# Forms of x made in the attention's output projection, and two more pairs of the feed-forward part computed by seven products

## The chip, the cores and the metric

The kernel runs on one core of one Trainium2 chip. The metric is the device time of one execution in microseconds (us). Times are medians of several runs; the profile comes from one execution, and its span reaches from the first to the last instruction.

The engines are named as the profile names them: PE is TensorE's matmul, PEld its weight load, DVE VectorE, ACT ScalarE, POOL GpSimd, SP the engine whose queue issues most loads. A name with a q (SPq, POOLq) is that engine's queue.

## The reference

Two layers work on one sequence of 512 tokens of 1024 features in float32. Each has a mixer (attention in layer 0, an mLSTM in layer 1), a cross-attention to a memory of 256 tokens, and a gated feed-forward part with a causal convolution of three taps. What bears on the change:

```python
def memory_cross_attention(xn, memn, wq, wkv, wo):
    q = split_heads(xn @ wq, XATTN_HEADS)
    k, v = jnp.split(memn @ wkv, 2, axis=-1)
    ...
    p = jax.nn.softmax(logits, axis=-1)
    out = jnp.einsum('bhqm,bhmd->bhqd', p.astype(v.dtype), v)
    return merge_heads(out) @ wo

def conv_ffn(xn, w_up, conv_w, conv_b, w_down):
    h = causal_depthwise_conv(xn @ w_up, conv_w) + conv_b
    g, u = jnp.split(h, 2, axis=-1)
    return (jax.nn.gelu(g) * u) @ w_down

    ...
        x = x + memory_cross_attention(rms_norm(x, xattn_norm[layer]), rms_norm(mem, mem_norm[layer]),
                                       xattn_wq[layer], xattn_wkv[layer], xattn_wo[layer])
        x = x + conv_ffn(rms_norm(x, ffn_norm[layer]), ffn_w_up[layer], ffn_conv_w[layer],
                         ffn_conv_b[layer], ffn_w_down[layer])
```

The inner width of the feed-forward part is 2816, so w_up makes 2 x 22 blocks of 128 features: 22 pairs of a gate block and an up block.

## The kernel before

**Products.** x lies with its features on the 128 partitions, in 8 tiles of 128 x 512. Every operand is split into a high part, rounded to the reduced float32 that TensorE reads (fp32r), and the low rest; a product is three matmuls, high by high, high by low and low by high (`mm3`, lines 347 to 349). So each 128 x 1024 slice of weights is loaded from memory (`raw`, three buffers), cast to its high part on ScalarE (`wh`) and subtracted to its low part on VectorE (`wl`; three buffers each). The profile shows all ScalarE, VectorE and GpSimd instructions under line 269, the wrapper that issues them, so they are told apart by their tiles.

**Cross-attention** (`xattn`). Keys (`kth`, `ktl`) and values (`xvh`, `xvl`) of the memory, four tiles of 8 KB a partition in the pool `xa`, are read by the scores and the weighted sums of four heads. Then `p_out` multiplies by the output weights in eight blocks m = 0 to 7 of 24 matmuls of 512 columns. After each, VectorE adds the block to x (`xadd`), ScalarE and VectorE make the high and low part of that x tile times the norm's gain (`xprep`: xh, xl) and add its squares for the next norm. A planner (`Plan`) sets the order of this part by priorities and assumed engine times.

**Feed-forward part** (`ffn_steps`). A planner (`Sched`) simulates the engines with assumed durations and fixes the order on TensorE, VectorE, ScalarE and GpSimd; SP's loads are placed by it, with loads allowed to run 14 us ahead, and are then issued in order by the queue. There are two ways to compute a pair:

- `plain`: gate block and up block, 8 slices of features each, 3 matmuls of 512 columns a slice: 48 matmuls. VectorE splits two weight tiles and evacuates two blocks times the norm.
- `seven`: the pair is a 2 x 2 product of blocks (gate and up by the two halves of the features, against the two halves of the features by the two halves of the tokens) computed with seven products of 256 columns in place of eight (4 slices x 3 matmuls each, 84 matmuls). It needs sums of weight blocks, which are made by loading and by adding transfers that GpSimd issues (`sa`, `sb`), one sum on VectorE, five splits of weights, and combinations of x, which are here called the forms: for feature tiles k and k + 4, T1 to T4 are differences of halves of both, 128 x 1024 together, split into `th` and `tl`. Results are combined in `hs` and multiplied by the norm.

After either, the `tail` runs the convolution (one ScalarE and two VectorE instructions a block), the gelu, the product and its split into `ah` and `al`. `SEVEN` (line 26) names the pairs by seven: 4 to 21 in both layers. The forms are made by `forms(k, at)` for k = 0 to 3, two after pair 0 and two after pair 1, with scratch in the tiles s2 and s4 and in `sa`; `th`, `tl` are 32 KB a partition in the pool `ff`. From pair 5 on, a pair by seven is interleaved with two fills (`fill`): blocks of the down projection of a chunk of earlier pairs, 12 matmuls of 512 columns each, whose results are added to x. The first fill uses pairs 0 to 3. Some fills are held back at the end (six in layer 0, four in layer 1), so the last pairs run without.

**Pools.** `xa` and `ff` follow each other in the same address range, and `mem`, which holds the output projection's operands of heads 2 and 3, lies at the start of the range that `ff` takes over. With `reuse_waits="tile"` a tile of the later pool waits only for the earlier tiles whose bytes it takes.

Of the kernel before, what the change touches and what calls it, by code (L numbers as in the profile page):

```python
# [1 line left out]

# [7 lines left out]
F32 = mybir.dt.float32  # L10
# [6 lines left out]
P = 128  # L17
# [8 lines left out]
SEVEN = (range(4, 22), range(4, 22))  # L26
# [269 lines left out]
class Builder:  # L296
# [25 lines left out]

    def acc_bank(self, b):
        return self.til(self.acc, f"acc{b}", bufs=1)
# [155 lines left out]
    def p_out(self, pl, src, mixed, kdeps, gain, gi, order, prio, reload=False, order0=None):  # L480

        state = {}
        done = []
        for m in range(KB8):
            e = self.p_proj(
                pl, src[m], mixed, lambda ps, m=m: self.xadd(m, ps, reload), (("D", 0.6),), kdeps=kdeps, order=order, prio=prio + m
            )
            done.append(
                pl.add(lambda m=m: self.xprep(m, gain, gi, state), 0, [e], prio + m, chain=(("A", 0.52), ("D", 0.66), ("A", 0.52)), order=[order0])
            )  # L490
        self.state = state
        self.xdone = {k: [d] for k, d in enumerate(done)}
# [634 lines left out]
    def xattn(self, layer):  # L1127
        nc, t, tc = self.nc, self.t, self.tc
        with tc.tile_pool(name=f"xa{layer}", bufs=1, reuse_waits="tile") as mp:
            self.mp = mp  # L1130
            pl = Plan(self.plan, [st["banks"][0] for st in self.fills], s=2, w=2, e=4, q=2, pt=2, wt=3)
            self.pad(mp, 192)
# [9 lines left out]
            for h in range(4):  # L1142
                p = 10 + 10 * h
                ke = []
                for m in (2 * h, 2 * h + 1):

                    def keys(ps, m=m, at=0):
                        tmp = self.til(mp, "tmp")
                        nc.vector.tensor_tensor(out=folded(tmp[:, :MEM]), in0=restored(ps[:, at : at + MEM]), in1=folded(self.memrb[:]), op=ALU.mult)
                        self.split(kth[:, m, :], ktl[:, m, :], tmp[:, :MEM])  # L1150
# [32 lines left out]
                if h % 2 == 0:  # L1183
                    cs = slice(256 * h, 256 * h + 512)

                    def values(tk, ps, cs=cs):
                        self.evac_tok(ps, self.memr[:, tk : tk + 1], vh[:, tk, cs], vl[:, tk, cs])
# [10 lines left out]
                for i in range(4):  # L1198
# [3 lines left out]
                    def score(h=h, qs=qs, res=res, sl=sl):  # L1202
                        sp = self.bank("s")
                        for d in range(2):
                            kb = 2 * h + d
                            self.mm3(sp[:, :MEM], qs[d][0][:, sl], qs[d][1][:, sl], kth[:, kb, :], ktl[:, kb, :], d == 0, d == 1)
# [22 lines left out]
                for d in range(2):  # L1229

                    def weigh(h=h, d=d, pts=pts):
                        c = slice(256 * h + P * d, 256 * h + P * d + P)
                        ps = self.bank("w")
                        for j in range(2):
                            self.mm3(ps[:], vh[:, j, c], vl[:, j, c], pts["h"][:, j, :], pts["l"][:, j, :], j == 0, j == 1)
# [7 lines left out]
            self.p_out(pl, t["xo"][layer], lambda: (mh, ml), kd, "ffn", layer, None, 100)  # L1243
# [8 lines left out]
    def ffn_steps(self, layer, mp):  # L1252
# [4 lines left out]
        sc = Sched(raw=3, h=3, s2=1, s4=1, a22=1, sa=3, sb=2, ra=2, hs=2, c=1, ft=2, v=1, u2=1, u3=1, act=10, acc=4, s=2, w=2)  # L1257
# [68 lines left out]
        add("DVE", 1.3, None, (), -20.0, after=1.8)  # L1326
        own = lambda k: (self.xh[k][:], self.xl[k][:])
# [32 lines left out]
        th, tl = ([mp.tile([P, 1024], F32R, name=f"t{i}{layer}{k}", tag=f"t{i}{k}") for k in range(4)] for i in "hl")  # L1360
        formed, pads = [], []
# [3 lines left out]

        def forms(k, at):

            st = {}

            def scaled(j):  # L1370
                st["t"] = st.get("t", ()) + (self.til(mp, ("s2", "s4")[st["_ft"]] + "hl"[j], bufs=1),)
                nc.scalar.activation(st["t"][j][:], self.x[k + 4 * j][:], AF.Identity, scale=self.col("ffn", layer * 8 + k + 4 * j))

            def first():
                st["r"] = raw_tile(st, "sa")[:]
                tt_(out=st["r"][:, T1], in0=st["t"][0][:, 0:256], in1=st["t"][0][:, 256:512], op=ALU.subtract)
                tt_(out=st["r"][:, T3], in0=st["t"][1][:, 256:512], in1=st["t"][0][:, 256:512], op=ALU.subtract)

            def second(to, a, b):
                nc.vector.scalar_tensor_tensor(out=st["r"][:, to], in0=st["r"][:, a], scalar=-1.0, in1=st["t"][1][:, b], op0=ALU.mult, op1=ALU.subtract)  # L1380

            T1, T3, T2, T4 = (slice(256 * i, 256 * i + 256) for i in range(4))
            tt_ = nc.vector.tensor_tensor
            a = add("ACT", ACV, lambda: scaled(0), (), at, [("ft", st)], after=X_LAST)
            a = add("ACT", ACV, lambda: scaled(1), [a], at)
            a = add("DVE", 2 * tt(256), first, [a], at, [("sa", st)])
            a = add("DVE", 0.4, lambda: second(T2, T1, slice(256, 512)), [a], at)
            a = add("DVE", 0.4, lambda: second(T4, T2, slice(0, 256)), [a], at, (), [("ft", st)])
            h = add("ACT", act(1024), lambda: nc.scalar.copy(th[k][:], st["r"]), [a], at)
            formed.append(add("DVE", tt(1024), lambda: self.sub(tl[k][:], st["r"], th[k][:]), [h], at, (), [("sa", st)]))  # L1390

# [66 lines left out]
        def seven(p, fill):  # L1458
# [75 lines left out]
            p6 = pe(n, lambda: product(s2, 0, *T2, "Y", False), [w2, v, *formed], (), [("s2", s2)])  # L1534
# [25 lines left out]
        def down(c, m, steps=1):  # L1560
# [22 lines left out]
            e = add("DVE", 0.6, lambda: self.xadd(m, d["ps"]), [last, xadded[m], *formed], clock[0] + 3.0, (), [("w", d)])  # L1583
# [10 lines left out]
        for p in range(22):  # L1594
# [6 lines left out]
            if p < 2:  # L1601
# [416 lines left out]
```

## Time and profile before

| | us |
|---|---|
| median of 3 runs | 1415.94 |
| lowest and highest | 1414.96, 1417.21 |
| the profiled execution's own time: its span, the only time that the profile gives of it | 1413.6 |
| median less span | 2.3 |
| TensorE busy | 1401.1 (99%) |
| VectorE busy | 1140.9 (81%) |
| ScalarE busy | 825.8 (58%) |
| GpSimd busy | 124.8 (9%) |
| moved | 190.02 MB, mean 134 GB/s |

Consecutive records of an engine overlap in the profile: a VectorE instruction's record ends after the next one has begun. Where pace matters, the distance from start to start is read, not the length of a record; busy times of a stage count overlapping time once. A matmul's record is longer than its pitch for the same reason, so small gaps of TensorE are found from starts and counts.

Layer 0's feed-forward part begins at 393.66 us and layer 1's at 1076.61 us.

### The profile page before, as it was taken

To read this page: it belongs to the slowest core of one execution; us is meant where nothing else is said; L and a number is where in the kernel's file an instruction comes from. 1 tells how busy PE (TensorE), PEld (TensorE's weight loads), DVE (VectorE), ACT (ScalarE), POOL (GpSimd) and SP (SyncE) were. 2 spreads that over 40 slices of the span, in tenths; PEclk is the share of its full clock that TensorE was granted. 3 is DMA by queue.
4 is the path that set the end of the run, shared out by engine and by line. 5 is a ranking of instruction groups with operands and counts; after the bars stand their busy time and mean duration, and the time that the engine had idled before them with its cause. 6 is when DMAs were issued, how large, how long until landed. Compare 5 with 4: busy or idle time off the path is not lost.

```text
span 1413.6 us, 22281 instructions
## 1 busy us (share of the span) xinstructions
PE 1401.1 (99%) x8448; PEld 1262.1 (89%) x8448; DVE 1140.9 (81%) x1922; ACT 825.8 (58%) x1386; POOL 124.8 (9%) x189
## 2 busy tenths in 40 slices
PE   9999999999999999999999999999999999999998
PEld 8888868899889999999888888989988999999997
DVE  7787886766699999999768876666667999999984
ACT  6797564444476656566446664445446656656655
POOL 0002220000001111110001121000000110111000
PEclk9999999999999999999999999999999999999999
DMA  5214324323258767774233332333323876767522
GB/s 206 90 55 155 112 83 147 123 81 129 89 155 211 195 179 185 183 177 114 77 114 102 129 97 83 121 102 120 120 82 134 202 205 169 193 172 189 141 76 81
DMA packets 69212, 190.02 MB, mean 134 GB/s; under 512 B 7553, under 2 KB 7553, under 8 KB 69105
## 3 DMA queue, kind: packets, MB, share of 16 engines
q1 hardware_dynamic: 55648, 153.48, 32.5%
q0 software_dynamic: 12448, 34.00, 13.6%
q8 instruction: 66, 1.08, 0.3%
q10 hardware_dynamic: 1008, 1.12, 0.2%
q14 instruction: 42, 0.34, 0.1%
HBM read 186.43 MB, written 2.15 MB: 133 GB/s over the span
## 4 chain that ended last, share of the span: by engine, by line
PE 88%; DVE 5%; ACT 3%; issue 2%; DMA 1%; POOL 0%; POOLq 0%; DVEq 0%; ACTq 0%
PE acc L347 18%; PE acc L348 18%; PE acc L349 17%; PE w L347 5%; PE w L349 5%; PE w L348 5%; PE s L347 3%; PE s L349 3%; PE s L348 3%; PE acc L409 2%; PE acc L411 2%; PE acc L410 2%; DVE wl L269 1%; PE w L1794 1%; PE w L1027 1%
## 5 line engine op out<-in xcount | busy, mean ns | idle before, releaser
L269 ACT CAST wh<-raw 128x1024 fp32r<-128x1024 f32 (+2 forms) x229 | 235.0, 1027 | 211.2 <-PE acc L348 114.0
L269 DVE TENSOR_TENSOR wl<-raw,wh 128x1024 fp32r<-128x1024 f32 (+2 forms) x229 | 273.8, 1197 | 43.6 <-ACT wh L269 42.9
L347 PE MATMUL acc<-xh,wh 128*128 128x512 f32 (+1 forms) x800 | 275.8, 345 | 0.0
L349 PE MATMUL acc<-xh,wl 128*128 128x512 f32 (+1 forms) x800 | 273.4, 342 | 0.0
L348 PE MATMUL acc<-xl,wh 128*128 128x512 f32 (+1 forms) x800 | 273.2, 342 | 0.0
L349 PEld LDWEIGHTS acc<-xh,wl 128*128 128x128 f32 x800 | 152.1, 190 | 13.7
L347 PEld LDWEIGHTS acc<-xh,wh 128*128 128x128 f32 x800 | 152.2, 190 | 12.6 <-DVE x L269 0.3
L348 PEld LDWEIGHTS acc<-xl,wh 128*128 128x128 f32 x800 | 152.2, 190 | 12.2
L269 DVE SCALAR_TENSOR_TENSOR c<-hs,vec,c 128x512 f32<-128x512 f32 x176 | 131.7, 748 | 3.8 <-ACT c L269 0.8
L347 PE MATMUL w<-ah,wh 128*128 128x512 f32 x304 | 115.7, 381 | 0.2 <-ACT c L269 0.2
L348 PE MATMUL w<-al,wh 128*128 128x512 f32 x304 | 115.2, 379 | 0.0
L349 PE MATMUL w<-ah,wl 128*128 128x512 f32 x304 | 115.2, 379 | 0.0
L269 ACT ACTIVATE c<-hs,vec 128x512 f32<-128x512 f32 x88 | 70.9, 812 | 10.3 <-DVE hs L269 5.9
L269 ACT CAST ah<-c 128x512 fp32r<-128x512 f32 x44 | 27.2, 618 | 83.8 <-DVE c L269 83.8
L269 DVE TENSOR_TENSOR x<-acc,x 128x512 f32<-128x512 f32 (+1 forms) x43 | 28.0, 652 | 56.3 <-PE acc L349 56.3
L347 PEld LDWEIGHTS w<-ah,wh 128*128 128x128 f32 x304 | 57.6, 190 | 7.9 <-DVE x L269 0.9
L349 PEld LDWEIGHTS w<-ah,wl 128*128 128x128 f32 x304 | 57.5, 189 | 8.1
L348 PEld LDWEIGHTS w<-al,wh 128*128 128x128 f32 x304 | 57.6, 190 | 6.5
L349 PE MATMUL acc<-mem,wl 128*128 128x256 f32 (+1 forms) x192 | 59.6, 310 | 1.1 <-DVE wl L269 1.1
L347 PE MATMUL acc<-mem,wh 128*128 128x256 f32 (+1 forms) x192 | 59.6, 310 | 0.1
L348 PE MATMUL acc<-mem,wh 128*128 128x256 f32 (+1 forms) x192 | 59.5, 310 | 0.0
L269 POOL DMA_DIRECT2D sa<-in_up_dram x36 | 31.8, 883 | 276.8 <-DMA sa<-in_up_dram 174.5
(365 smaller groups left out, 3762.0 us busy)
## 6 DMA issues: line engine op xcount, KB each, us to landing
raw<-in_up_dram SPq DMA_DIRECT2D x52, 512.0 KB, 3.9
sa<-in_up_dram SPq DMA_DIRECT2D x36, 512.0 KB, 3.4
sa<-in_up_dram POOLq DMA_DIRECT2D x36, 512.0 KB, 6.5
raw<-in_down_dram SPq DMA_DIRECT2D x32, 512.0 KB, 3.8
ra<-in_up_dram SPq DMA_DIRECT2D x36, 256.0 KB, 4.0
sb<-in_up_dram POOLq DMA_DIRECT2D x36, 256.0 KB, 4.8
raw<-in_wo_dram SPq DMA_DIRECT2D x16, 512.0 KB, 3.9
raw<-in_xk_dram SPq DMA_DIRECT2D x16, 512.0 KB, 3.3
```

The costliest lines, as they stand in the source:

```text
L269: i = issue(*a, **k)
L347: mm(out, wh, xh, start=first, stop=False, skip_group_check=parts)
L348: mm(out, wh, xl, start=False, stop=False, skip_group_check=parts)
L349: mm(out, wl, xh, start=False, stop=last, skip_group_check=parts)
L409: mm(ps, xh[k][:, ts], wh, start=(k == 0), stop=False)
L410: mm(ps, xh[k][:, ts], wl, start=False, stop=False)
L411: mm(ps, xl[k][:, ts], wh, start=False, stop=(k == 7))
L1027: nc.tensor.matmul(ps[64 * s : 64 * s + 64, j * P : 512], v[j][:, c : c + 64], pts[s]["t"][:, at : at + 512 - j * P], start=(j == 0), stop ...
L1794: nc.tensor.matmul(ps[:, lo:], vv[s][:, c], a[:], start=(s == 0), stop=(s == 3))
```

## The change

- Keys, values and forms share one pool `far`, placed from the other end of the memory: eight tiles of 128 x 1024 (`far_tiles`). Keys and values are sliced out of them; when the attention has read them, the same tiles are asked for again for `th` and `tl`. The four old tiles of `xa` and the eight of `ff` go, and three paddings with them.
- `p_out` of the cross-attention takes its blocks in the order 0, 4, 1, 5, 2, 6, 3, 7 and makes the form of tiles k and k + 4 (`form`) as soon as both are done, with scratch in `tmp` and `pth` of the attention's pool. The instructions of a form are the same as before: two scalings, four differences, a cast and a subtraction.
- `forms` in the feed-forward part goes; the planner there counts the last form as work that is already under way.
- Pairs 2 to 21 instead of 4 to 21 are computed by seven.
- `finish` takes its output tiles from `far`.

```diff
-SEVEN = (range(4, 22), range(4, 22))
+SEVEN = (range(2, 22), range(2, 22))
...
+    def far_tiles(self):
+
+        return [self.til(self.far, f"f{i}", (P, 1024), F32R, bufs=1) for i in range(8)]
...
-    def p_out(self, pl, src, mixed, kdeps, gain, gi, order, prio, reload=False, order0=None):
+    def p_out(self, pl, src, mixed, kdeps, gain, gi, order, prio, reload=False, order0=None, forms=None):
...
-        for m in range(KB8):
+        for n, m in enumerate((0, 4, 1, 5, 2, 6, 3, 7) if forms else range(KB8)):
...
+            done[m] = pl.add(lambda m=m: self.xprep(m, gain, gi, state), 0, [e], prio + n, chain=(("A", 0.52), ("D", 0.66), ("A", 0.52)), order=[order0])
+            if forms and m >= 4:
+                if m == 4:
+                    self.forms = [None] * 4
+                pl.add(
+                    lambda k=m - 4: self.form(forms, gi, k), 0, [done[m - 4], done[m]], prio + n,
+                    chain=(("A", 1.22), ("D", 1.4), ("A", 0.95), ("D", 1.14)),
+                )
...
+    def form(self, pool, layer, k):
+
+        nc = self.nc
+        if k == 0:
+            self.far_forms = self.far_tiles()
+        hi, lo = self.far_forms[2 * k : 2 * k + 2]
+        v = [self.til(pool, "tmp"), self.til(pool, "tmp")]
+        for j in range(2):
+            nc.scalar.activation(v[j][:], self.x[k + 4 * j][:], AF.Identity, scale=self.col("ffn", layer * 8 + k + 4 * j))
+        r = self.til(pool, "pth", (P, 2, 512), F32R)[:].rearrange("p a b -> p (a b)").bitcast(F32)
+        T1, T3, T2, T4 = (r[:, 256 * i : 256 * i + 256] for i in range(4))
+        x0, x1 = ([v[j][:, 256 * i : 256 * i + 256] for i in range(2)] for j in range(2))
+        nc.vector.tensor_tensor(out=T1, in0=x0[0], in1=x0[1], op=ALU.subtract)
+        nc.vector.tensor_tensor(out=T3, in0=x1[1], in1=x0[1], op=ALU.subtract)
+        nc.vector.scalar_tensor_tensor(out=T2, in0=T1, scalar=-1.0, in1=x1[1], op0=ALU.mult, op1=ALU.subtract)
+        nc.vector.scalar_tensor_tensor(out=T4, in0=T2, scalar=-1.0, in1=x1[0], op0=ALU.mult, op1=ALU.subtract)
+        self.split(hi[:], lo[:], r)
+        self.forms[k] = hi, lo
...
-            kth = mp.tile([P, KB8, MEM], F32R, name=f"kth{layer}")
-            ktl = mp.tile([P, KB8, MEM], F32R, name=f"ktl{layer}")
-            self.pad(mp, 64)
-            vh = mp.tile([P, 2, DM], F32R, name=f"xvh{layer}")
-            vl = mp.tile([P, 2, DM], F32R, name=f"xvl{layer}")
+            tiles = self.far_tiles()
+            kt = lambda part, m: tiles[2 * part + m // 4][:, m % 4 * MEM : m % 4 * MEM + MEM]
+            vt = lambda part, j, c: tiles[4 + 2 * part + j][:, c]
...
-            self.p_out(pl, t["xo"][layer], lambda: (mh, ml), kd, "ffn", layer, None, 100)
+            self.p_out(pl, t["xo"][layer], lambda: (mh, ml), kd, "ffn", layer, None, 100, forms=mp)
...
+        f = add("ACT", 1.22, None, (), -20.0, after=2.4)
+        f = add("DVE", 1.4, None, [f], -20.0)
+        f = add("ACT", 0.95, None, [f], -20.0)
+        formed = add("DVE", 1.14, None, [f], -20.0)
...
-        th, tl = ([mp.tile([P, 1024], F32R, name=f"t{i}{layer}{k}", tag=f"t{i}{k}") for k in range(4)] for i in "hl")
-        formed, pads = [], []
+        th, tl = zip(*self.forms)
+        pads = []
...
-            p6 = pe(n, lambda: product(s2, 0, *T2, "Y", False), [w2, v, *formed], (), [("s2", s2)])
+            p6 = pe(n, lambda: product(s2, 0, *T2, "Y", False), [w2, v, formed], (), [("s2", s2)])
...
-            if p < 2:
-                for k in (2 * p, 2 * p + 1):
-                    forms(k, clock[0] + 4.0 * (k % 2))
...
-                with tc.tile_pool(name=f"mem{layer}", bufs=1, reuse_waits="tile") as self.memp:
-                    (self.mix0, self.mix1)[layer]()
-                    self.xattn(layer)
-                self.ffn(layer)
+                with ExitStack() as right:
+                    with tc.tile_pool(name=f"mem{layer}", bufs=1, reuse_waits="tile") as self.memp:
+                        (self.mix0, self.mix1)[layer]()
+                        self.far = right.enter_context(tc.tile_pool(name=f"far{layer}", bufs=1, side="right", reuse_waits="tile"))
+                        self.xattn(layer)
+                    self.ffn(layer)
```

More of the change, by code (lines that the diff above doesn't have):

```diff
@@ L1 @@
 import math
+from contextlib import ExitStack
 import numpy as np
@@ L1364, in ffn_steps @@
             nc.gpsimd.memset(h[:, :, 0:2], 0.0)
[L1366 to L1390, printed above, removed]
         def tail(p, st, deps, at):
@@ L1582, in down @@
                     joined([last], last.prio, [("act", acted[first + k].st)])
-            e = add("DVE", 0.6, lambda: self.xadd(m, d["ps"]), [last, xadded[m], *formed], clock[0] + 3.0, (), [("w", d)])
+            e = add("DVE", 0.6, lambda: self.xadd(m, d["ps"]), [last, xadded[m]], clock[0] + 3.0, (), [("w", d)])
             xadded[m] = e
@@ L1847, in finish @@
         HALF = [slice(0, 256), slice(256, 512)]
-        outs = [self.til(mp, f"t{i}{k}", (P, 1024), F32R, bufs=1).bitcast(F32)[:, s] for k in range(4) for i in "hl" for s in (slice(0, 512),)]
+        outs = [v[:].bitcast(F32)[:, 0:512] for v in self.far_tiles()]
         def add(m, ps, c):
```

20 lines of the change are left out of this document (8 added, 12 removed).

## The prediction

> **What bounds the kernel now.** I read the page first, then the busy time by stage, then TensorE's and VectorE's timelines at the start of layer 0's feed-forward part, then the chain of waits at its end.
>
> ```profile
> span 1413.6 us, 22281 instructions
> PE 1401.1 (99%) x8448; PEld 1262.1 (89%) x8448; DVE 1140.9 (81%) x1922; ACT 825.8 (58%) x1386; POOL 124.8 (9%) x189
> ...
> PE 88%; DVE 5%; ACT 3%; issue 2%; DMA 1%; POOL 0%; POOLq 0%; DVEq 0%; ACTq 0%
> ```
>
> TensorE is busy for 99% of the span and 88% of the chain that ended last is its own work, so shortening it should show, if what feeds it keeps up. That is read stage by stage. The columns are the stage, its length, and each engine's busy time with its instructions; one to three matmuls of the stage before reach into each row. The stages are: four blocks of the attention's output projection, the whole start of the feed-forward part up to the first down-projection block (layer 0, then layer 1), three plain pairs, the first stretch by seven products, and in layer 0's end the last pairs and what follows them.
>
> ```profile
> core 0: us, PE busy (x) PEld busy (x) DVE busy (x) ACT busy (x) POOL busy (x), PEclk, DMA share, GB/s
> 372.94:393.66 20.72, 20.72 (x97) 18.14 (x96) 12.72 (x16) 8.78 (x13) 0.00 (x0) 1.00 0.36 127
> ...
> 405.35:436.43 31.08, 31.08 (x146) 27.22 (x145) 30.34 (x45) 18.47 (x24) 3.54 (x4) 1.00 0.75 200
> 436.43:449.82 13.39, 13.39 (x121) 13.39 (x120) 12.94 (x20) 9.89 (x16) 2.58 (x3) 1.00 0.92 243
> 393.66:449.82 56.16, 56.16 (x323) 50.95 (x322) 54.52 (x84) 38.80 (x54) 7.30 (x8) 1.00 0.70 191
> ...
> 644.48:667.26 22.78, 22.78 (x207) 22.78 (x206) 22.22 (x33) 16.46 (x28) 1.72 (x2) 1.00 0.34 90
> 667.26:720.46 53.20, 53.04 (x267) 45.99 (x266) 42.11 (x63) 24.13 (x38) 1.13 (x3) 1.00 0.29 91
> ...
> 1076.61:1132.77 56.16, 56.16 (x323) 50.95 (x322) 54.52 (x84) 38.80 (x54) 7.17 (x8) 1.00 0.69 183
> ```
>
> The granted clock is 1.00 throughout. TensorE has no idle time at the start of the feed-forward part, in either layer, but VectorE has only 56.16 - 54.52 = 1.64 us to spare there. In the output projection VectorE has 8.00 us free in 20.72. The change moves VectorE work from the first place to the second and puts other VectorE work in its place, so there are two accounts to make: TensorE's gain, and whether VectorE can still hide.
>
> **TensorE's gain.** These rows of its timeline are the first matmul of the feed-forward part, of pair 1 (plain, like 0, 2 and 3), of pair 4 (by seven) and of the first down-projection block.
>
> ```profile
> 393.66 0.38 PE L347 MATMUL acc<-xh,wh 128*128 128x512 f32 x1
> ...
> 405.35 0.38 PE L347 MATMUL acc<-xh,wh 128*128 128x512 f32 x1
> ...
> 436.43 0.27 PE L347 MATMUL acc<-xh,wh 128*128 128x256 f32 x1
> ...
> 449.82 0.38 PE L347 MATMUL w<-ah,wh 128*128 128x512 f32 x1
> ```
>
> Pairs 1 to 3 are 3 x 2 blocks x 8 x 3 = 144 matmuls of 512 columns in 31.08 us: 215.8 ns each, 10.36 us a pair. From 436.43 to 449.82 run ten products of 4 x 3 = 12 matmuls of 256 columns: 13.39 / 120 = 111.6 ns each. A pair by seven has 84 of them, 9.37 us. The gain is 0.99 us a pair, 1.97 a layer; the two layers make 3.9 us.
>
> A rule against it: the Trainium skill, "TensorE: Matmul & The Clock Gate", section "Back-to-back issue gap", gives 262 and 518 cycles for 256 and 512 columns, which at its 2.4 GHz would make the gain 1.19 us a pair, 4.8 in all. The same section has sustained streams with weight loads at about 81 ns for 128 columns and 131 ns for 512; by that, seven products would cost at least 84 x 81 = 6.8 us against 48 x 131 = 6.3, a loss. The 111.6 and 215.8 ns of the rows agree with neither fully: near the first, far from the second.
>
> **The forms of x: 2.6 us of VectorE each.** A form is two scalings (ScalarE), four differences of 256 columns and one 1024-wide subtraction (VectorE), and one 1024-wide cast (ScalarE). VectorE's timeline has one, from 397.73 to 401.80, and ScalarE's the same one; an instruction's pitch is its start to the next start.
>
> ```profile
> 395.86 0.74 DVE L269 SCALAR_TENSOR_TENSOR xl<-x,vec,xh 128x512 fp32r<-128x512 f32 x1
> 396.53 0.68 DVE L269 TENSOR_TENSOR sq<-sq,sqt 128x512 f32<-128x512 f32 x1
> 397.13 0.68 DVE L269 TENSOR_TENSOR a22l<-ra,a22h 128x512 fp32r<-128x512 f32 x1
> 397.73 0.41 DVE L269 TENSOR_TENSOR sa<-s2h 128x256 f32<-128x256 f32 x1
> 398.07 0.41 DVE L269 TENSOR_TENSOR sa<-s2l,s2h 128x256 f32<-128x256 f32 x1
> 398.40 0.88 DVE L269 SCALAR_TENSOR_TENSOR sa<-sa,s2l 128x256 f32<-128x256 f32 x2
> 399.20 0.42 DVE L269 TENSOR_TENSOR sa<-s4h 128x256 f32<-128x256 f32 x1
> ...
> 400.66 1.22 DVE L269 TENSOR_TENSOR tl<-sa,th 128x1024 fp32r<-128x1024 f32 x1
> 401.80 0.16 DVE L269 CAST rh<-y 128x4 fp32r<-128x4 f32 x1
> ```
> ```profile
> 396.25 0.72 ACT L269 ACTIVATE s2h<-x,vec 128x512 f32<-128x512 f32 x1
> 396.87 0.71 ACT L269 ACTIVATE s2l<-x,vec 128x512 f32<-128x512 f32 x1
> 397.49 0.70 ACT L269 ACTIVATE s4h<-x,vec 128x512 f32<-128x512 f32 x1
> ...
> 399.32 1.04 ACT L269 CAST th<-sa 128x1024 fp32r<-128x1024 f32 x1
> 400.27 1.04 ACT L269 CAST wh<-raw 128x1024 fp32r<-128x1024 f32 x1
> ```
>
> Four differences take 399.20 - 397.73 = 1.47, the subtraction 401.80 - 400.66 = 1.14: 2.61 us a form. Three of four move wholly into the output projection; the fourth needs the last block of x, so it still runs after the feed-forward part has begun. In the projection they add 7.83 us over eight blocks, where four blocks alone leave 8.00 free: costed at nothing. Without that cover they would cost up to 2 x 7.83 = 15.7 us. ScalarE's share, 2 x 0.62 and 0.95, so 2.19 us a form, lies in the 11.94 us that it has free in the same row.
>
> **What replaces them.** By the same pitches (0.60 for 512 columns, 0.34 for 256, 1.14 for 1024, 0.67 for the three-operand 512), a plain pair asks of VectorE two weight subtractions 2.28, two evacuations 1.20, and the tail: four taps, a product and a subtraction, 3.88; 7.36 in all. A pair by seven asks 2 x 1.14 + 3 x 0.60 for its five splits, 0.60 for the summed weights, 3 x 0.34 for evacuations, 1.14 for the scaling by the norm and the same tail: 10.72. The difference is 3.36 a pair, 6.72 for pairs 2 and 3.
>
> So at the start of each feed-forward part VectorE's work becomes 54.52 - 7.83 + 6.72 = 53.41 us, in 56.16 - 1.97 = 54.19 us of TensorE: 0.78 us to spare instead of 1.64. It still fits, with half the room. It is also less even: pairs 2, 3 and 4 run without fill, each with 10.72 us of VectorE work against 9.37, 1.35 over, 4.05 in all; what is put off is the tails, and the first deadline for those is the first down-projection block (449.82 before), which needs pair 3's. Layer 0's end bounds the price from above: the last three pairs also run without fill, and there VectorE is what TensorE waits for.
>
> ```profile
> 655.76 1.13 DVE wl L269
> ...
> 674.02 1.14 DVE wl L269
> ...
> 682.43 0.76 DVE c L269
> ```
>
> From 667.26 to 720.46 there are 48 matmuls of 256 columns and 216 of 512: 5.36 + 46.61 = 51.97 us of work in 53.20, so 1.23 us lost. At that end nothing can be put off; at the start the tails can, and pair 4 by seven without fill costs TensorE nothing in either layer today. The bounds are 0 and 1.2 us a layer; I take 0, by the nearer row.
>
> **Loads and tiles.** Two more pairs by seven a layer bring four added transfers each on SP's queue and GpSimd's. These rows are the page's shares of the 16 engines' span, its times from issue to landing, and SP's queue around the boundary at 393.66.
>
> ```profile
> q1 hardware_dynamic: 55648, 153.48, 32.5%
> q0 software_dynamic: 12448, 34.00, 13.6%
> ...
> raw<-in_up_dram SPq DMA_DIRECT2D x52, 512.0 KB, 3.9
> ...
> sa<-in_up_dram POOLq DMA_DIRECT2D x36, 512.0 KB, 6.5
> ...
> sb<-in_up_dram POOLq DMA_DIRECT2D x36, 256.0 KB, 4.8
> ```
> ```profile
> 380.44 10.69 SPq L1285 DMA_DIRECT2D raw<-in_up_dram  x3
> ...
> 395.97 0.33 SPq L1285 DMA_DIRECT2D raw<-in_up_dram  x1
> ...
> 404.53 4.46 SPq L1285 DMA_DIRECT2D raw<-in_up_dram  x2
> ```
>
> q1 takes 1413.6 x 0.325 / 153.48 = 2.99 us of all engines per MB, q0 5.65. A plain pair reads 1.05 MB, 3.1 us; a pair by seven 1.31 MB on SP and 0.79 MB added from GpSimd, 8.4 us. The stretch of 56.16 us at a share of 0.70 holds 39.3 us of transfers; 2 x 5.3 more make 49.9 in 54.2, a share of 0.92. That is the most a stage shows today, and part of it is fetched ahead for later pairs, so it can slip; I cost it at nothing.
>
> The tiles decide when it may begin. The first tiles of a pair by seven (sa) now come at the front of a pool that takes over the attention's space, where the projection's operands are read until 393.66 and the last form's scratch until about 401.9 (the end of today's first form, which starts from the same block of x). SP works in order: a load that waits for such a tile holds back the plain loads queued behind it, and pair 1's last weights leave at 395.97 today. If they leave only at 401.9, they land at 405.8 by the 3.9 row and are split by 408.0 (cast and subtraction, 1.04 and 1.22); they are needed at 405.35 + 5.18 = 410.5. That is nothing lost. With two 512 KB transfers served ahead of them, 1.6 us each by the 2.99, it is 0.6 us, and with the engines at 0.92 perhaps twice that, 1.2 us a layer. I take 0. The second half of pair 2's weights in raw leaves at 404.53 as today, lands at 408.4, is summed and split by about 411, and GpSimd's last addition lands at about 416 (4.8); it is wanted after five products, at 415.7 + 5 x 1.34 = 422.4.
>
> Where keys, values and forms lie costs TensorE nothing: operands from three pools (the projection row's 96 matmuls in 20.72 us, the plain row's 144 in 31.08) have one pitch of 215.8 ns.
>
> **The sum.** The profiled execution spans 1413.6 us, the median of the runs is 1415.94, 2.3 more. 1413.6 - 3.9 = 1409.7 for the span, and 1412.0 for the time: -0.28%. About 0.2% (2.8 us) is what a measurement of this kernel can tell from no change, so losses of 1.1 us would hide the gain.
>
> **The rivals.** *VectorE sets the pace of pairs 2 to 4* (slower). Place: the three pairs without fill. If it enters pair 2 with nothing in hand, TensorE waits the whole 1.35 us three times in both layers, 8.1 us: 1412.0 + 8.1 = 1420.1. It decides from the point where the 0.78 us to spare turn negative, that is, if some 0.8 us more VectorE work than I count falls between the first matmul and the first down block. For: 54.52 of 56.16 and layer 0's end. Against: the start holds as much today without a gap.
>
> *Part of it is lost* (no change). Either VectorE costs 1.2 us a layer as at layer 0's end, or the weights of pair 1 come 1.2 us late in each behind a waiting sa load: 1414.4 for one of them, 1416.8 for both.
>
> *More than counted* (faster): the 1.23 us at layer 0's end also goes, since the same work comes to it in another order: 1410.8.
>
> *Short matmuls are dear* (slower): if a matmul of 256 columns cost 0.62 of one of 512, 133 ns, a pair by seven would take 11.2 us, 0.9 more than a plain one, and 3.4 in all: 1419.3. The 111.6 ns of 36 pairs' rows speak against it. The ratio of 81 to 131 in the section named above is 0.62.
>
> *The change does nothing*: TensorE's order could be held by the fourth form, which every pair by seven needs. It ends near 401.9 and pair 2 starts at 405.35 + 10.36 = 415.7, so this would need 13 us of delay; its chance is in the second rival's.
>
> **How the numbers follow.** Forecast 0.60, with its own range 1411.2 to 1413.1; VectorE's pace 0.12; part lost 0.22; more than counted 0.05; dear matmuls 0.01. Faster 0.65, same 0.22, slower 0.13. The range 1410.6 to 1416.0 leaves out the slower cases (0.13), a little of the part lost (0.03) and below (0.02).
>
> **What would show it.** Right: 2 x 2 x 48 = 192 matmuls of 512 columns fewer and 2 x 2 x 84 = 336 of 256 more; the first down block 54.2 us after the feed-forward part's first matmul in both layers, VectorE near 99% between, form instructions in the gaps before 393.7, and pitch 111.6 ns in pairs 2 and 3. Wrong: gaps of TensorE inside pairs 2 to 5 or ahead of the first down block, released by VectorE (its pace); a gap ahead of pair 1's second block or pair 2, released by a weight subtraction whose load left late (the loads); or an output projection longer than 5.18 us a block (the forms not hidden).

## The result, and the profile after

The changed kernel takes 1435.68 us (median of 4 runs, 1432.67 to 1437.22), the kernel before 1415.45 us in the same comparison: a ratio of 1.0139, interval 1.0127 to 1.0151. The forecast was 1412.0 us, faster. The sign was wrong. One execution among all the runs, of the kernel before with pairs 2 to 21 by seven, took 2892.17 us and is left out of that run's figures.

From the page of the changed kernel: the span, the engines' busy time, and the shares of the chain of work that ended last.

```profile
span 1433.6 us, 22671 instructions
PE 1407.8 (98%) x8592; PEld 1269.7 (89%) x8592; DVE 1152.1 (80%) x1946; ACT 836.1 (58%) x1414; POOL 133.9 (9%) x197
PE 81%; DVE 9%; issue 3%; ACT 3%; DMA 2%; POOL 0%; DVEq 0%; POOLq 0%; SPq 0%; ACTq 0%
```

TensorE issues 8592 - 8448 = 144 matmuls more, as foreseen, but its own share of the chain falls from 88% to 81%. The next rows are stages of the changed kernel (columns as in the prediction): layer 0's and layer 1's feed-forward part up to the first down block, layer 0's first 20 us, a stretch in which TensorE is mostly idle, and the three stretches after such waits, at half the clock (the third in two rows).

```profile
393.54:460.73 67.19, 61.68 (x420) 57.27 (x418) 53.93 (x80) 38.23 (x61) 11.75 (x14) 0.95 0.78 204
1085.41:1152.84 67.43, 61.30 (x419) 57.24 (x418) 54.12 (x80) 38.33 (x61) 11.69 (x14) 0.95 0.80 204
393.54:413.54 20.00, 17.70 (x86) 15.26 (x85) 9.89 (x18) 6.02 (x8) 4.80 (x6) 1.00 0.94 257
410.05:413.46 3.41, 1.11 (x6) 0.60 (x4) 2.43 (x6) 0.29 (x1) 1.75 (x1) 1.00 1.06 236
413.46:416.88 3.42, 3.42 (x10) 2.79 (x9) 2.05 (x3) 1.53 (x2) 0.91 (x1) 0.50 0.58 168
427.12:430.53 3.41, 3.41 (x17) 3.22 (x16) 3.41 (x5) 1.55 (x3) 0.00 (x0) 0.50 0.78 132
1116.61:1120.02 3.41, 2.64 (x10) 2.33 (x11) 3.41 (x6) 2.59 (x4) 0.87 (x1) 0.50 0.02 6
1120.02:1123.44 3.42, 3.42 (x18) 3.42 (x18) 3.08 (x5) 2.00 (x4) 0.29 (x1) 0.50 1.00 151
```

The first down block comes 67.2 and 67.4 us after the first matmul, not 54.2. Some 2.7 us of that is order: two products, 24 matmuls of 256 columns at 111.6 ns, stand ahead of it now that stood behind it (the stage has 420 matmuls, one or so at its edges, where 323 + 168 - 96 = 395 were foreseen). So 56.9 would have been without loss, and 10.3 and 10.5 us are lost. The span grew by 20.0 us while TensorE's work shrank by 3.9; 20.8 of these 23.9 us are lost here. And VectorE, the engine that was to run out of time, does only 9.89 us of work in the first 20, where the kernel before has it do 19.22 (the prediction's start of the feed-forward part, read over its first 20 us):

```profile
393.66:413.66 20.00, 20.00 (x98) 17.64 (x97) 19.22 (x35) 15.81 (x22) 1.18 (x1) 1.00 0.42 142
```

What VectorE waited for is in its own timeline, with ScalarE's, GpSimd's and SP's beside it (changed kernel, layer 0; in brackets the idle time before the instruction and what ended it).

```profile
399.33 1.23 DVE L270 TENSOR_TENSOR f<-pth,f 128x1024 fp32r<-128x1024 f32 x1 [1.11 <-ACT f L270]
403.58 0.69 DVE L270 TENSOR_TENSOR a22l<-ra,a22h 128x512 fp32r<-128x512 f32 x1 [3.03 <-ACT a22h L270]
409.00 0.69 DVE L270 TENSOR_TENSOR sb<-sa,raw 128x512 f32<-128x512 f32 x1 [4.72 <-DMA sa<-in_up_dram]
409.61 0.15 DVE L270 TENSOR_SCALAR z<-s 128x4 f32<-128x4 f32 x1
409.68 1.22 DVE L270 TENSOR_TENSOR wl<-raw,wh 128x1024 fp32r<-128x1024 f32 x1
```
```profile
402.93 0.62 ACT L270 CAST a22h<-ra 128x512 fp32r<-128x512 f32 x1 [3.64 <-DMA ra<-in_up_dram]
...
414.42 0.59 ACT L270 COPY rb<-s 128x512 f32<-128x512 f32 x1 [4.08 <-PE s L570]
414.90 1.05 ACT L270 CAST wh<-raw 128x1024 fp32r<-128x1024 f32 x1
```
```profile
401.14 0.94 POOL L270 DMA_DIRECT2D sa<-in_up_dram  x1 [7.22 <-DMA sa<-in_up_dram]
...
409.85 1.96 POOL L270 TENSOR_TENSOR y<-z,power 128x4 f32<-128x4 f32 x1 [3.17 <-DVE z L270]
```
```profile
381.32 14.86 SPq L1311 DMA_DIRECT2D raw<-in_up_dram  x4
396.23 2.43 SPq L1311 DMA_DIRECT2D sa<-in_up_dram  x2
```

The last form of x ends at 400.6. Then VectorE stands for 3.0 us before pair 2's ra split (a22l) and for 4.7 us before its weight sum (sb), whose sa load left at 396.2 and had GpSimd's addition to follow. Each of these engines takes its instructions in the order in which they were written, so everything behind stands too: the first step of the norm (z), which runs at 400.3 where nothing holds it (first experiment), and pair 1's last weight subtraction (wl). GpSimd's power (y) and ScalarE's copy of the spread norm (rb) follow z. TensorE stops where these are missing (its waits in layer 0, from 390 to 465):

```profile
PE s L570 <- DVE sqt L270: 2.3, 1, 2.3
PE acc L352 <- ACT wh L270: 1.9, 1, 1.9
PE acc L352 <- ACT u L270: 0.9, 1, 0.9
```

Two of these are followed by the half-clock stretches above: 3.42 + 3.41 us in layer 0, 6.83 in layer 1, with TensorE busy for 12.9 of the 13.7. At half speed 6.4 us of that is lost, a quarter of the loss.

That gives theory A: the order written by the planner lets pair 2's loads start up to 14 us before the feed-forward part, so pair 2's work stands at the heads of three queues ahead of the norm and of pair 1, while the loads really leave at 396. The rivals: B, VectorE is short of time; C, the DMA engines are full; D, the forms in the projection or the new places of the tiles cost something. Except where a run says otherwise, the edits are to the changed kernel. All ratios are to the kernel before on the same chip.

### The profile page after: what moved, and what is told of

Its sections match the earlier page's. It is cut to its first block, busy times and chain, and to the rows that moved or that the text cites. A ratio compares the mean times of both kernels' runs of the same rounds, so it can differ in the third digit from the quotient of the medians.

```text
span 1433.6 us, 22671 instructions
## 1 busy us (share of the span) xinstructions
PE 1407.8 (98%) x8592; PEld 1269.7 (89%) x8592; DVE 1152.1 (80%) x1946; ACT 836.1 (58%) x1414; POOL 133.9 (9%) x197
## 4 chain that ended last, share of the span: by engine, by line
PE 81%; DVE 9%; issue 3%; ACT 3%; DMA 2%; POOL 0%; DVEq 0%; POOLq 0%; SPq 0%; ACTq 0%
PE acc L352 15%; PE acc L353 15%; PE acc L354 15%; PE w L352 5%; PE w L354 5%; PE w L353 5%; PE acc L414 3%; PE acc L416 3%; PE acc L415 3%; PE s L352 3%; PE s L354 2%; PE s L353 2%; DVE wl L270 2%; DVE c L270 2%; DMA sa<-in_up_dram 1%
## 5 line engine op out<-in xcount | busy, mean ns | idle before, releaser
L270 ACT CAST wh<-raw 128x1024 fp32r<-128x1024 f32 (+2 forms) x225 | 230.8, 1027 | 182.4 <-PE acc L353 91.9
L270 DVE TENSOR_TENSOR wl<-raw,wh 128x1024 fp32r<-128x1024 f32 (+2 forms) x225 | 269.0, 1197 | 44.8 <-ACT wh L270 43.9
L352 PE MATMUL acc<-xh,wh 128*128 128x512 f32 (+1 forms) x768 | 262.5, 342 | 4.9 <-ACT wh L270 4.3
L353 PE MATMUL acc<-xl,wh 128*128 128x512 f32 (+1 forms) x768 | 259.0, 337 | 0.0
L354 PE MATMUL acc<-xh,wl 128*128 128x512 f32 (+1 forms) x768 | 258.7, 337 | 0.0
L352 PEld LDWEIGHTS acc<-xh,wh 128*128 128x128 f32 x768 | 147.3, 192 | 16.8 <-ACT wh L270 4.7
L354 PEld LDWEIGHTS acc<-xh,wl 128*128 128x128 f32 x768 | 146.9, 192 | 12.1
L353 PEld LDWEIGHTS acc<-xl,wh 128*128 128x128 f32 x768 | 147.4, 192 | 10.6
L270 ACT CAST ah<-c 128x512 fp32r<-128x512 f32 x44 | 27.3, 620 | 67.4 <-DVE c L270 67.4
L270 POOL DMA_DIRECT2D sa<-in_up_dram x40 | 35.0, 901 | 248.1 <-DMA sa<-in_up_dram 106.3
```

What stands on the lines that cost most here:

```text
L270: i = issue(*a, **k)
L352: mm(out, wh, xh, start=first, stop=False, skip_group_check=parts)
L353: mm(out, wh, xl, start=False, stop=False, skip_group_check=parts)
L354: mm(out, wl, xh, start=False, stop=last, skip_group_check=parts)
```

## Experiments: is it the order?

**The planner told when the loads can start.** In `load` of the feed-forward part:

```diff
-            return add("SP", 0.0017 * cols, fn, (), at, [(tag, st)], (), 4.0)
+            return add("SP", 0.0017 * cols, fn, (), at, [(tag, st)], (), 4.0, -99.0 if tag == "raw" else 2.5)
```

> Edit: the planner that writes the order of the feed-forward part is told that the loads into sa, sb and ra tiles can't begin before 2.5 us after TensorE's first matmul there; nothing else is changed, so the instructions and their waits are the same and only their planned order differs. Theory A (order): the 20 us are lost because pair 2's ra split and weight sum stand in VectorE's and ScalarE's queues ahead of the norm's scaling and of pair 1's weight subtraction, and wait there until 409.0 for an sa load that could not leave before 401.1. Planned later, they stand behind that work: first down block 55 to 58 us after the first matmul in both layers (67.2 now), time 1412 to 1418 us. Theory B (VectorE is short of time in pairs 2 to 4): the same work in the same time, 1430 us or more. Theory C (the DMA engines are full, share 0.92): the weights still come when they come, 1428 us or more. Theory D (the forms delay the loads in the projection): no change, 1430 or more.

Measured: 1417.54 us, ratio 1.0020 (1.0011 to 1.0030). 18 of the 20 us are back, with the same work. VectorE's timeline in this run, GpSimd's and ScalarE's:

```profile
400.31 0.15 DVE L270 TENSOR_SCALAR z<-s 128x4 f32<-128x4 f32 x1
400.38 1.22 DVE L270 TENSOR_TENSOR wl<-raw,wh 128x1024 fp32r<-128x1024 f32 x1
...
406.82 1.23 DVE L270 TENSOR_TENSOR wl<-raw,wh 128x1024 fp32r<-128x1024 f32 x1 [2.74 <-ACT wh L270]
...
411.81 0.68 DVE L270 TENSOR_TENSOR sb<-sa,raw 128x512 f32<-128x512 f32 x1
```
```profile
400.55 1.93 POOL L270 TENSOR_TENSOR y<-z,power 128x4 f32<-128x4 f32 x1 [6.78 <-DVE z L270]
402.44 0.93 POOL L270 DMA_DIRECT2D sa<-in_up_dram  x1
```
```profile
405.26 0.58 ACT L270 COPY rb<-s 128x512 f32<-128x512 f32 x1 [5.18 <-PE s L570]
```

z runs at 400.3 instead of 409.6, and rb at 405.3 instead of 414.4. The sum (sb) still runs late, at 411.8, but nothing urgent stands behind it. The DMA share of the first 20 us is 0.93 here and 0.94 in the changed kernel, so C falls as the cause of these 18 us, and so does B.

**The tiles elsewhere.** Tiles of the feed-forward pool are requested in another order, so that sa and ra lie where the projection reads nothing.

```diff
+        for tag, n, dtype, bufs in (("ah", 512, F32R, 10), ("sa", 1024, F32, 3), ("c", 1024, F32, 1), ...):
+            self.til(mp, tag, ..., dtype, bufs=bufs)
```

> Edit: in the changed kernel's feed-forward pool the tiles are laid down in another order, so that the sa and ra tiles come to lie where the attention's queries and probabilities lay, which are read for the last time well before the projection ends, and not over operands that the projection reads until 393.7. The planned order of every queue stays as in the changed kernel. Theory A in its first form (the loads are late because of the tiles): the sa load leaves well before 393, lands before 399, the weight sum waits little, and most of the loss goes: 1412 to 1418 us. Theory A in a second form (the sa loads stand in SP's order behind plain loads that are themselves late): the sa load still leaves after 396 and half or more of the loss stays, 1422 to 1434. Theory B (VectorE short of time): 1430 or more. Theory C (full DMA engines): 1428 or more, or worse since more is in flight at once.

Measured: 1433.83 us, 1.0131 (1.0116 to 1.0146). SP's queue in this run:

```profile
380.94 14.86 SPq L1311 DMA_DIRECT2D raw<-in_up_dram  x4
395.85 0.94 SPq L1311 DMA_DIRECT2D sa<-in_up_dram  x2
```

The first sa load leaves only 0.4 us earlier. It isn't its tile that holds it, but the plain loads ahead of it on SP, the last of which leaves at 395.8. The second did wait for its tile in the changed kernel, 1.6 us, and doesn't here, but that gives back no more than the noise allows to be told. This is A in its second form.

**The first half of the change alone**, pairs 2 and 3 plain (`SEVEN = (range(4, 22), range(4, 22))`), then the same with the loads planned as in the first run.

> Edit: the changed kernel, with its forms in the projection and the shared pool, but pairs 2 and 3 plain as before; this is the first half of the change alone. Theory A: no sa tile is wanted before pair 4, so nothing waits at the head of a queue; 1414 to 1417 us, the kernel before within 0.1%, with VectorE some 46.7 us busy in the 56.2 us before the first down block. Theory D (forms in the projection delay what follows): 1425 us or more. Theories B and C say the same as A here.

Measured: 1421.32 us, 1.0043 (1.0028 to 1.0058): a miss for A as I had put it, since pair 4's ra split already does the same harm. VectorE's timeline in this run:

```profile
404.68 0.69 DVE L270 TENSOR_TENSOR a22l<-ra,a22h 128x512 fp32r<-128x512 f32 x1 [4.27 <-ACT a22h L270]
```

> Edit: the run with pairs 2 and 3 plain (forms in the projection, shared pool) and the planner told that the loads into sa, sb and ra tiles begin no earlier than 2.5 us. The run without that word lost 4.6 us of span against the kernel before; there a ra split stands at the head of VectorE's queue from 400.3 to 404.7, and pair 4 is late at 440. Theory A (order): the loss is the same one in small, and goes: 1414 to 1416 us, TensorE without a wait at 440. Theory D (forms in the projection or where the tiles lie cost by themselves): 1419 us or more as without it.

Measured: 1415.66 us, 1.0000 (0.9991 to 1.0010). D falls: forms and tiles cost nothing by themselves that a run shows. The stage up to the first down block in both runs, without and with the planned loads:

```profile
393.39:451.92 58.53, 56.98 (x323) 51.30 (x322) 47.04 (x69) 31.30 (x44) 6.85 (x10) 1.00 0.67 186
```
```profile
392.87:449.03 56.16, 56.16 (x323) 50.95 (x322) 48.20 (x70) 31.89 (x44) 8.24 (x10) 1.00 0.74 203
```

## Experiments: which queue?

**The weight sum moved behind the norm.**

```diff
-            b2 = add("DVE", tt(512), s2_, [b1, l2], at - 5.0, [("sb", sb)])
+            b2 = add("DVE", tt(512), s2_, [b1, l2, normed], at - 5.0, [("sb", sb)])
```

> Edit: in a pair by seven the weight sum (sb from sa and raw) is planned to follow the feed-forward norm; in the first pair this puts it behind the norm's scaling in VectorE's order. Loads, tiles and the ra split stay where they are. Theory A: the norm's scaling no longer waits until 409.6 for the sa load, and neither do pair 1's second weight subtraction (409.7) and the load behind it; most of the loss goes, 1412 to 1422 us, the upper end if the ra split (held until 403.6) alone still costs pair 1 some us. Theories B (VectorE short of time), C (full DMA engines) and D (forms): 1430 us or more, since one instruction's place changes neither the work nor the transfers.

Measured: 1431.20 us, 1.0114 (1.0099 to 1.0129). A miss: 4.5 us back, not most.

**The ra split moved as well** (`w22 = split(a22, 512, [l1, normed], ...)`).

> Edit: in the changed kernel both the weight sum (sb from sa and raw) and the split of the ra weights are planned to follow the norm, so neither can stand in VectorE's or ScalarE's order ahead of the norm's work and pair 1's last weights; SP's order is left to the planner as in the changed kernel. The run with the sum alone moved gave back 4.5 us; there the ra split held VectorE to 403.7 and, through the two ra tiles, SP until 405.9. Theory A (waiting instructions at the head of in-order queues): most of the rest goes, 1415 to 1421 us, near the run with the loads planned later. Theory C (full DMA engines): 1428 or more. If SP's own order (ra loads and sa loads ahead of the next plain load) is the larger part: 1422 to 1430.

Measured: 1431.45 us, 1.0112 (1.0097 to 1.0127), a miss again. GpSimd's timeline shows a further queue that holds the norm, and ScalarE's shows the copy:

```profile
401.05 0.94 POOL L270 DMA_DIRECT2D sa<-in_up_dram  x1 [7.61 <-DMA sa<-in_up_dram]
403.22 0.85 POOL L270 DMA_DIRECT2D sa<-in_up_dram  x1 [1.23 <-DMA sa<-in_up_dram]
405.01 0.84 POOL L270 DMA_DIRECT2D sa<-in_up_dram  x1 [0.94 <-DMA sa<-in_up_dram]
405.57 1.35 POOL L270 TENSOR_TENSOR y<-z,power 128x4 f32<-128x4 f32 x1
```
```profile
410.99 0.58 ACT L270 COPY rb<-s 128x512 f32<-128x512 f32 x1 [11.22 <-PE s L570]
```

z runs at 400.0, but GpSimd's power stands behind three additions that wait for sa loads. rb comes at 411.0 instead of the first run's 405.3.

**GpSimd's power moved ahead of the additions**, with the two moves above, and then alone.

```diff
+            state["power"] = b
...
-            b1 = onto(..., [b1, summed.get(p - 2) if p == 6 else None], at - 16.0)
+            b1 = onto(..., [b1, summed.get(p - 2) if p == 6 else None, state["power"]], at - 16.0)
```

> Edit: the run with the weight sum and the ra split planned behind the norm, and in addition GpSimd's additions onto sa planned behind the norm's power on GpSimd. Without the last, GpSimd's order was three sa additions (401.1, 403.2, 405.0, each waiting for an sa load) and then the norm's power at 405.6, though its operand was ready at 400.1; so rb came at 411.0 instead of 405.3, and ScalarE's and VectorE's work on pair 2's weights stood behind it. Theory A carried to GpSimd: this wait alone was what was left, and the time comes to 1416 to 1420 us, as with the loads planned later. If the remaining loss has another cause (sa loads ahead on SP, the DMA engines at 0.9): 1426 us or more.

Measured: 1418.31 us, 1.0022 (1.0012 to 1.0031), as A expected.

> Edit: in the changed kernel GpSimd's additions onto sa are planned behind the norm's power on GpSimd; since the weight sum needs them, it moves behind the norm as well. The ra split stays at the head of VectorE's and ScalarE's queues, waiting for its load until about 404. If GpSimd's order is nearly the whole price: 1418 to 1421 us. If the ra split, through the two ra tiles and SP's next plain load (405.9 instead of 401.3), costs 4 us a layer by itself: 1424 to 1428 us.

Measured: 1431.17 us, 1.0107 (1.0092 to 1.0122), above both expectations. The ra split holds z to 403.4 here, 3.1 us later than in the first run, but rb comes 4.8 us later:

```profile
405.79 0.68 DVE L270 TENSOR_TENSOR sqt<-ident,rl 128x512 fp32r<-128x512 f32 x1
```
```profile
410.11 0.59 ACT L270 COPY rb<-s 128x512 f32<-128x512 f32 x1 [6.37 <-PE s L570]
```

The operand of the spread (sqt) is ready at 406.5, and TensorE, without a wait, makes the second of its two matmuls (s) at 409.69. So TensorE's own order holds the norm as well. Counted from the feed-forward part's first matmul, the spread stands behind 56 matmuls in the first run and with all three moves, the two runs that have the time back. Its two matmuls stand behind 82 and 85 in the changed kernel and in the runs with the sum moved and with the ra split moved as well, and behind 79 and 82 here. With each of these edits the planner writes a new order for every engine, and no run moves the spread alone. So the parts don't add, and what one queue keeps by itself isn't shown. What is shown is that the three runs in which rb comes 5 to 6 us later than in the first all keep some 13 us.

## Experiments: what is left

**Pairs 3 to 21 by seven**, loads planned as in the first run.

> Edit: as the run with the loads planned from 2.5 us, but with pairs 3 to 21 by seven and pair 2 plain. That run still loses 2.9 us a layer against the kernel before in the stretch from 420 to 540, with VectorE busy for 99% of it. Theory B in small (VectorE's pace is what is left): one pair by seven fewer takes 3.4 us of VectorE work a layer away and the loss goes to under 1 us a layer, while TensorE's gain halves to 2.0 us: 1413.5 to 1415.5 us. If what is left is not VectorE's pace (DMA engines 0.91 busy, or TensorE's order), the loss shrinks little and the time is 1416.5 us or more.

Measured: 1416.31 us, 1.0006 (0.9996 to 1.0015), above what B expected and not clearly of the other case. Layer 0's and layer 1's stage up to the first down block:

```profile
393.68:448.86 55.18, 55.18 (x359) 51.26 (x358) 48.97 (x72) 34.86 (x52) 9.29 (x12) 1.00 0.81 216
1076.52:1131.70 55.18, 55.18 (x359) 51.26 (x358) 48.94 (x72) 34.86 (x52) 9.63 (x12) 1.00 0.80 216
```

Here the gain of a pair arrives whole in each layer, 55.18 against 56.16, and TensorE never waits in these stages. The median doesn't show these 2.0 us. In the trace 0.5 us of it goes to a longer wait in layer 1's mixer (1.1 us for hsq against 0.6); where the rest goes isn't settled.

**The scaling by the norm left out**, in pairs 2 and 3, then in pairs 2 to 7, on top of the planned loads.

```diff
+                if p > 3:
                     tt_(out=h, in0=h, in1=self.rb[:]..., op=ALU.mult)
```

> Edit: the run with the loads planned from 2.5 us, with the scaling by the norm left out for pairs 2 and 3 (one VectorE instruction of 1.14 us each, so two a layer; the output lacks the norm there), its planned place kept. Theory B in small (VectorE's pace sets the 2.9 us a layer that are left): 2.3 us of VectorE work a layer less give back about as much, 1412.5 to 1414.5 us, and the 1.1 us wait ahead of pair 5's sixth product (450.2) goes. If the loads or the DMA engines set it: 1416.5 to 1418, as without the edit.

Measured: 1415.74 us, 0.9998 (0.9989 to 1.0007), between the two expectations.

> Edit: the run with the loads planned from 2.5 us, with the scaling by the norm left out for pairs 2 to 7 (six VectorE instructions of 1.14 us a layer, 6.8 us; the output lacks the norm there), their planned places kept. The same for pairs 2 and 3 alone gave 1.8 us back. If VectorE's pace is what is left of the loss: 1411.5 to 1413.5 us, the forecast of 1412.0, with no wait of TensorE over 0.3 us from 390 to 520. If part of it lies in loads or transfers: 1414.5 to 1416 us.

Measured: 1412.01 us, 0.9976 (0.9966 to 0.9986). Stages of the run with the scaling: the first 20 us and what follows up to the first down block. Then the whole stage of the run without it:

```profile
393.38:413.38 20.00, 20.00 (x98) 17.66 (x97) 14.85 (x25) 11.50 (x15) 4.74 (x6) 1.00 0.93 257
413.38:451.65 38.27, 37.30 (x323) 36.76 (x322) 37.68 (x55) 26.89 (x46) 6.93 (x8) 1.00 0.89 223
```
```profile
393.79:450.82 57.03, 57.03 (x419) 54.32 (x418) 49.84 (x77) 38.06 (x60) 10.85 (x13) 1.00 0.90 239
```

Even in the good order VectorE is busy for only 14.85 of the first 20 us, and then for 37.68 of 38.27. With 6.8 us a layer taken away TensorE has no gap there, and the time is the forecast's, though of a kernel that does less work. So what the good order still loses, 5.5 us in two layers, goes with VectorE's work (B in small).

**The scaling on GpSimd instead**, for pairs 2 to 7 and, with pair 2 plain, 3 to 7.

> Edit: the run with the loads planned from 2.5 us, with the scaling by the norm of pairs 2 to 7 on GpSimd instead of VectorE (1.14 us of VectorE each, 6.8 us a layer). If VectorE's pace is what that run still loses: 1412 to 1415 us. If GpSimd is slow at it (a power of 4 columns takes it 1.35 to 1.95 us, and no run shows 1024 columns) and the tails and the additions wait for it: 1417 us or more.

> Edit: the run with pairs 3 to 21 by seven and the loads planned from 2.5 us, with the scaling of pairs 3 to 7 on GpSimd (5.7 us of VectorE a layer). VectorE's pace: 1412.5 to 1415 us. GpSimd slow at it or in the way: 1416 us or more.

Measured: 1423.83 us, 1.0058 (1.0043 to 1.0073), and 1421.09, 1.0041 (1.0028 to 1.0054). GpSimd takes 2.5 us for it (the first run, pair 2) where VectorE takes 1.14, and both times lie in the upper case, slower than without the edit:

```profile
428.88 2.49 POOL L270 TENSOR_TENSOR hs<-hs,rb 128x1024 f32<-128x1024 f32 x1 [4.37 <-DVE hs L270]
```

**The second half of the change alone**: the kernel before, pairs 2 to 21 by seven, loads planned as in the first run.

> Edit: the kernel before (forms of x made after the feed-forward part has begun, tiles as before) with pairs 2 to 21 by seven and the loads of sa, sb and ra planned from 2.5 us; this is the second half of the change without the first. By the prediction's account VectorE then has 54.5 + 6.7 = 61.2 us of work in 54.2 us of TensorE, 7.0 us too much in each layer. If VectorE's pace is the price of pairs by seven at the start: 5 to 7 us a layer, 1422 to 1428 us. If VectorE's work can be put off without price: 1413 to 1417, and the forms needn't have moved.

Measured: 1435.36 us, 1.0141 (1.0121 to 1.0161), more than either case. TensorE's longest wait in layer 0, and what GpSimd's first addition waits for:

```profile
PE s L347 <- ACT wh L269: 3.8, 1, 3.8
```
```profile
410.06 0.94 POOL L269 DMA_DIRECT2D sa<-in_up_dram  x1 [9.43 <-DVE sa L269]
```

The old forms use the sa tiles as scratch, so pair 2's sa loads take their turn behind them. The run shows that pairs 2 and 3 by seven want the forms out of the way; how much of its 20 us is VectorE's pace it doesn't tell.

## Why the prediction was wrong

*TensorE's gain* held: 0.98 us a pair and layer in the run from pair 3, and 1412.01 us with the scalings of six pairs a layer left out.

*The forms of x* held: they cost nothing in the projection (the feed-forward part begins at 393.54 us, at 393.66 before), and the first half of the change with its loads planned is the kernel before to 0.1%.

*Loads and tiles* is the step that failed. It had the place right (sa loads that leave late) and followed only what is queued behind them on SP: pair 1's plain weights, "nothing lost". It never asked what stands behind the instructions that wait for these loads, on VectorE, ScalarE and GpSimd, nor where the planner would then put the norm's spread on TensorE. What stood there was the norm and pair 1's last subtraction, and this order cost 1435.68 - 1417.54 = 18 us. The tile as the cause of the first late load was wrong too; it was SP's order. So was the reading of SP's rows. raw has three buffers, so a load waits for the subtraction of the third weights before its own. The load of 395.97 follows that of pair 1's first block, which ends at 395.95, so it brings pair 2's second; pair 1's last had left at 385.6. Taking GpSimd's additions as harmless because their sums are wanted late missed that GpSimd also serves the norm. The mark named for this, a gap ahead of pair 2's weights, is in the trace, with the norm's spread ahead of it.

*What replaces them* had the total right (53.41 us foreseen, 52.53 measured in the good order) and its place wrong. The forms had filled VectorE's time at the start; without them 5.15 of the first 20 us stay empty, and the work that came instead doesn't move there. In the first run the first sum's transfer lands at 411.0. Pair 2's first plain weights land at 396.9, but ScalarE casts them only at 405.74, behind rb and after TensorE has left pair 0, and VectorE stands 2.74 us for that cast. "0.78 us to spare" supposed that the work could move. The term was put at 0, with bounds of 0 and 1.2 us a layer, and measured 2.8 (5.5 / 2) in the good order.

Of *the rivals*, VectorE's pace was the right one for those 5.5 us, for another reason than the one given. *Short matmuls are dear* fell with TensorE's gain; so did the ratio of 81 to 131 that the Trainium skill, "TensorE: Matmul & The Clock Gate", section "Back-to-back issue gap", gives (111.6 to 215.8 ns in these traces). The DMA share foreseen, 0.92, came (0.90 up to the first down block in the run with the loads planned) and cost nothing that a run shows.

## What to carry to other kernels

A load that is late costs what stands behind its users on every in-order engine, so list for each new wait the queue behind it on all of them, TensorE's too. Don't add up prices of waits that run side by side: here the edits that freed some of the queues gave back 4.5 of 18 us. A planned order is only as good as the start times that the planner was given; when tiles, loads or buffers move, correct those first. Work taken out of a stretch is room only for work whose inputs are ready by then.

## What was not expected of the hardware

The same wait can cost two different amounts. In the run with GpSimd's power moved alone, TensorE waits 2.87 us for the same weights (wh) in both layers. The first two rows hold layer 0's wait, the others layer 1's and what follows it:

```profile
417.53:420.94 3.41, 1.79 (x14) 1.41 (x12) 3.38 (x6) 1.59 (x2) 0.34 (x1) 1.00 0.79 268
420.94:424.35 3.41, 1.79 (x16) 1.79 (x17) 3.41 (x6) 3.41 (x5) 1.36 (x2) 1.00 0.61 117
1107.02:1110.43 3.41, 1.56 (x12) 1.19 (x10) 3.38 (x6) 1.58 (x3) 0.57 (x1) 1.00 0.81 268
1110.43:1113.84 3.41, 2.02 (x9) 2.02 (x10) 3.41 (x6) 3.33 (x5) 0.69 (x2) 0.50 0.53 111
1113.84:1117.25 3.41, 3.41 (x18) 3.41 (x17) 3.15 (x5) 2.04 (x4) 0.71 (x2) 0.50 0.82 199
```

After the first the clock stays at 1.00; after the second it is 0.5 for 6.8 us, in which TensorE is busy for 5.4 and so loses 2.7 us on top of the wait. The Trainium skill, "TensorE: Matmul & The Clock Gate", section "What's actually happening", has the clock decided in windows of 3413 ns that run free of the kernel. The half-clock stretches of 3.41, 3.42 and 6.83 us agree with it, and the rows above are cut on that grid, from the end of the half clock at 1117.25 backwards: both waits cross an edge of it. The first, from 419.7 to 422.6, leaves the windows on both sides 1.79 us busy, 52%. The second, from 1108.9 to 1111.8, leaves the window in which it begins 1.56 us busy, 46%, and at the end of that window, within the wait, the clock falls. The section has the clock fall after an idle window; here windows busy for 1.11 us (410.05 to 413.46 in the changed kernel) and 1.56 us were enough. Where the bound lies isn't shown, nor that busy time is what counts: in the run with pairs 3 to 7 scaled on GpSimd the clock falls after a window busy for 2.25 us, 66% (823.16 to 826.57), in which eight of the matmuls are two columns wide.
